# State-space layer: table reads issued from two queues, transposes and GLU items in another order, more filling products

## Chip, core and metric

One NeuronCore of one Trainium2 chip computes a two-layer decoder trunk in a single launch. The metric is the device time of one execution in microseconds (us), as a median of several runs. The engines are TensorE (PE, with its weight loads as PEld), VectorE (DVE), ScalarE (ACT), GpSimd (POOL) and SyncE (SP, which issues the DMA transfers). Each works through its own queue in order and waits for the others by semaphores.

## What is computed

Layer 0 mixes the 512 positions with a diagonal complex state-space layer (64 groups of 16 channels, 64 states each), layer 1 with stick-breaking attention. Each mixer is followed by a layer norm, a dense SwiGLU block and another layer norm. All is float32. The change lies in layer 0's mixer:

```python
def s5_mixer(x, a_re, a_im, log_dt, b_re, b_im, c_re, c_im, d_skip, w_glu, w_out):
    ...
    _, _, s_re, s_im = lax.associative_scan(
        _ssm_combine, (a_seq_re, a_seq_im, bu_re, bu_im), axis=0)
    y = (jnp.einsum('lbgp,ghp->blgh', s_re, c_re.astype(f32))
         - jnp.einsum('lbgp,ghp->blgh', s_im, c_im.astype(f32)))
    y = y.reshape(bsz, seq, D_MODEL) + d_skip.astype(f32) * x.astype(f32)
    h = jax.nn.gelu(y).astype(x.dtype)
    val, gate = jnp.split(h @ w_glu, 2, axis=-1)
    z = val * jax.nn.sigmoid(gate)
    return (z @ w_out).astype(x.dtype)
```

## The kernel before

Layer 0's mixer is `ssm` (L460), and `ssm_end` (L897) finishes its GLU and output projection. The scan over 512 positions is cut into 64 chunks of 8. The 64 groups are handled in four blocks, 0 to 3, of 16 groups (two halves of 8). The instructions of all engines are issued in an order written out by hand, the string `SSM_ORDER` (L61), inside a manual schedule (L875): each word is one step, its first letter the kind and its digit the block. Every engine executes its own instructions in just that order. For one block b:

- **c** (L607): two short copies on ACT that put tables into PSUM bank 1. **g**, **j** (`f_g`, L624): DVE's outer products with B, two halves. **h**, **i** (`f_h`, L629): the same with C. Each half is three DVE operations over 1024 columns.
- **t**, **T** (`p_t`, L634): eight PE transposes of one half of g, and two ACT copies to SBUF, each of one bank. t uses banks 0 and 2, T uses banks 0 and 3. **m**, **M** (`p_m`, L646): PE products of x with the transposed tables, into banks 2 and 3.
- **e** (`f_e`, L713): POOL builds rotation tables (six operations, one into a scratch tile "eu"), ACT one copy. **r** (L735) and **s** (L747): DVE rotates m's result, scans it, rotates back.
- **k** (`p_k`, L667): PE products that give the convolution tables, two ACT copies, and two DMAs that write them to DRAM. **n** (`f_n`, L701): 16 DMAs from SP read them back in shifted form: eight for the block's first eight groups, eight for the others. n needs k's write.
- **y** (`p_y`, L763): PE products of tables and states into banks 6 and 7, a group pair after the other; the first four pairs read only the first half of n's tables. Two ACT copies. **z** (`p_z`, L787): eight PE transposes of that result in banks 6 and 7, GELU on ACT (two operations), and ACT's high part xh. **l** (`f_l`, L801): DVE's low part xl.
- **d9** (`p_d`, L657): nine products of the identity with itself, into bank 7, which nobody reads. They only keep PE at work.
- **u** (`glu_some`, L856): the next item of `GLU_FIRST` (L57): part of the product h @ w_glu on PE in banks 6 (value) and 7 (gate), and two ACT copies that keep it (`glu_keep`, L826). An item "30" is output chunk 3 with input quarter 0 (the rows of block 0); "001" is chunk 0 with quarters 0 and 1, so twice as long. Quarter b needs block b's xh and xl. **w0**, **w4** do the last two items of the list and leave them in PSUM. **a** (`glu_add`, L831) adds kept parts pairwise on POOL.
- **p**, **q** (`pump`, L865): split the next weight chunk into a high part (ACT) and a low part (POOL for p, DVE for q, L231), free its raw buffer, and issue from SP the load of a chunk three further on.

Every tile of 128 x 1024 is taken from a ring of 37 buffers (`Ring`, L160): `get` takes the buffer that has been free the longest in program order, `put` appends one to that list. A new tile waits until the last reader of the former tile in its buffer is done, on whatever engine that is. So the order of the words also decides which tile waits for whom.

In the order before, block 3's h takes the buffer of e3's scratch "eu". The words around it are `u1 u1 u1 a p e3 s2 g3 y2 t3 j3 z2 T3 m3 M3 h3 p u1 i3 p l2 k3 n3 r3 u1 u1 p s3 q y3`.

Of the kernel before, what the change touches and what calls it, by code (L numbers as in the profile page):

```python
# [45 lines left out]
def glu_items(text):  # L46
# [12 lines left out]


SSM_ORDER = (  # L61
# [3 lines left out]
)  # L65

TNX = {0: 0, 1: 1, 2: 0}
# [177 lines left out]
class Trunk:  # L245
# [214 lines left out]
    def ssm(self):  # L460


        tc, nc, io, ring, ws = self.tc, self.nc, self.io, self.ring, self.ws
# [52 lines left out]
        for hf in range(4):  # L516
# [4 lines left out]
        kd = dr.tile([NBLK, 16, 32, 240], F32, name="kd")  # L521
# [4 lines left out]
                          in_=zero.unsqueeze(1).to_broadcast([128, NBLK * 4, 112]))  # L526
# [33 lines left out]
        nr, den, t1, t2, t3, t4, cfr, cfi = (small(n) for n in ("nr", "den", "t1", "t2", "t3", "t4", "cfr", "cfi"))  # L560
        l1, l2 = small("l1"), small("l2")
# [39 lines left out]
        h3 = lambda t, i: t[:, i * 512:(i + 1) * 512].rearrange("p (j c) -> p j c", j=GB)  # L601
# [99 lines left out]
        def f_n(b):  # L701
            if b in TNX:
                half = (self.xl, self.xh)[TNX[b]][:, 4:8].rearrange("p k t -> p (k t)").bitcast(F32)
                tn = [half[:, :1024], half[:, 1024:]]
            else:
                tn = [ring.get("tn", F32) for _ in range(2)]
            for hf in range(2):
                for n in range(L):
                    nc.sync.dma_start(out=tn[hf][n * 16:(n + 1) * 16].rearrange("p (g t) -> p g t", g=8),
                                      in_=kd[b, hf * 8:hf * 8 + 8, 0:16, n * 16:n * 16 + 128].rearrange("g h t -> h g t"))  # L710
            st[b]["tn"] = tn

        def f_e(b):  # L713
# [90 lines left out]

        part, zt = {}, [None] * 8

        def glu(i, qs, banks, start=True, stop=True):

            w = []
            for q in qs:  # L810
                c, half = self.c_glu[i, q]
                hl = ws.get(c, 0)
                w.append([t[:, half * 512:(half + 1) * 512].rearrange("p (k v m) -> p k v m", k=2, v=2) for t in hl])
            for v in (1, 0):
                for n, q in enumerate(qs):
                    for k in range(2):
                        kt = 2 * q + k
                        self.mm3(self.ps[:, banks + v], w[n][0][:, k, v], w[n][1][:, k, v], self.xh[:, kt], self.xl[:, kt],
                                 n == 0 and k == 0 and start, n == len(qs) - 1 and k == 1 and stop)
            for q in qs:  # L820
                c, half = self.c_glu[i, q]
                if half == 1:
                    ws.done(c)

        def glu_keep(i, banks):
            t = ring.get("part", F32)  # L826
            for v in (1, 0):
                nc.scalar.activation(t[:, v * S:v * S + S], self.ps[:, banks + v], AF.Copy)
            part.setdefault(i, []).append(t)

# [24 lines left out]
        def glu_some(n):  # L855
            for _ in range(n):  # L856
                i, qs = first.pop(0)
                glu(i, qs, 6)
                glu_keep(i, 6)

        def rest(banks):
            i, qs = first.pop(0)
            glu(i, qs, banks, stop=False)

        def pump(e):  # L865
# [4 lines left out]
        fs = dict(c=a_c, g=f_g, j=lambda b: f_g(b, 1), h=f_h, i=lambda b: f_h(b, 1), d=p_d, t=p_t,  # L870
                  T=lambda b: p_t(b, 1), m=p_m, M=lambda b: p_m(b, 1), e=f_e, k=p_k, r=f_r, y=p_y, l=f_l,
                  L=lambda b: f_l(b, G_), n=f_n, s=f_s, z=p_z,
                  B=lambda b: (powers(rest_), G_.memset(scr[0][:, 0:1], 0.0), scr_done()), b=lambda b: (levels(rest_), scr_done()))
        ET = mybir.EngineType
        with tc.manual_schedule(engines={ET.PE, ET.DVE, ET.Activation, ET.Pool, ET.SP}):  # L875
            for w in SSM_ORDER.split():
                if w[0] == "u":
                    glu_some(1)
                elif w[0] == "w":
                    rest(int(w[1]))  # L880
                elif w == "x":
                    ws.load(2)
                elif w == "a":
                    glu_add()
                elif w in "pq":
                    pump(G_ if w == "p" else V)
                else:
                    fs[w[0]](int(w[1]))
# [4 lines left out]
        nc.sync.dma_start(out=self.xres, in_=io["x_rev"])  # L893
        self.ln_load(io["ln_mix_g"][0], io["ln_mix_b"][0])
        self.glu, self.glu_end, self.zt = glu, glu_end, zt

    def ssm_end(self, nxt):  # L897
# [349 lines left out]
```

## Time and profile before

| | us |
|---|---|
| median of 3 runs (lowest to highest) | 1248.86 (1248.78 to 1250.04) |
| the profiled execution | 1248.96 |
| its span from first to last instruction | 1247.2 |
| PE busy | 1191.5 |
| DVE, ACT, POOL busy | 666.4, 422.6, 190.5 |

The trace is that of one execution. Its times count from the start of the span; what the device time has beyond the span is the time around it. A timeline row gives an instruction's start and duration, the engine, the line, what it writes and reads, how many were merged, and in brackets how long the engine stood idle before it and what released it. The state-space part takes about the first 205 us; the fields of the table by stretches stand in its header row.

### The profile page before, as it was taken

The page shows a single profiled execution, that of the slowest core. Times are in us where ns is not written, and L with a number is a line of the kernel's source. Part 1 is how long each engine was busy: PE and PEld are TensorE (multiplying, and loading weights), DVE is VectorE, ACT ScalarE, POOL GpSimd, SP SyncE. Part 2 cuts the span into 40 slices and gives each one's busy share as a digit, 9 for nine tenths or more (in the row PEclk, how much of TensorE's full clock was granted, in tenths as well). Part 3 has the DMA queues.
Part 4 walks back from the last instruction along what each step waited for, and adds up shares of the span by engine and source line. Part 5 has one row for each costly group of instructions (what it writes and reads, how often), then busy time and mean ns, then how long its engine had stood idle before and what let it go on. Part 6 is the DMA issues. An engine that isn't in the chain of part 4 may idle for free.

```text
span 1247.2 us, 16906 instructions
## 1 busy us (share of the span) xinstructions
PE 1191.5 (96%) x6964; PEld 989.7 (79%) x6964; DVE 666.4 (53%) x1033; ACT 422.6 (34%) x601; POOL 190.5 (15%) x212
## 2 busy tenths in 40 slices
PE   3799999999999999999999999999999999999996
PEld 2577688898888888888887888878888888888885
DVE  8975666643323333234867787868433333333236
ACT  1355263142222222222246666653222223332200
POOL 6636302120000000001312222224200000000000
PEclk9899999999999999999999999999999999999998
DMA  5333453142222223442201122133322222234301
GB/s 192 111 94 92 144 195 112 37 149 69 85 85 85 85 84 106 148 136 84 85 7 63 52 68 62 58 101 122 133 85 85 85 85 85 69 117 152 102 17 51
DMA packets 44781, 117.66 MB, mean 94 GB/s; under 512 B 6816, under 2 KB 18080, under 8 KB 44576
## 3 DMA queue, kind: packets, MB, share of 16 engines
q1 hardware_dynamic: 44704, 116.59, 29.3%
q8 instruction: 54, 0.88, 0.3%
q14 instruction: 23, 0.19, 0.1%
HBM read 112.51 MB, written 4.06 MB: 93 GB/s over the span
## 4 chain that ended last, share of the span: by engine, by line
PE 83%; DVE 9%; ACT 3%; POOL 2%; issue 1%; DMA 1%; SPq 1%; DVEq 0%; POOLq 0%; ACTq 0%
PE psum L294 17%; PE psum L292 17%; PE psum L293 16%; PE psum L313 8%; PE psum L312 8%; PE psum L311 8%; PE psum L776 2%; DVE nb L1015 2%; PE psum L1037 1%; DVE h L466 1%; ACT wh L228 1%; DVE wl L231 1%; PE psum L1102 1%; PE psum L1053 1%; PE psum L687 1%
## 5 line engine op out<-in xcount | busy, mean ns | idle before, releaser
L292 PE MATMUL psum<-xh,wh 128*128 128x512 f32 (+1 forms) x1056 | 394.6, 374 | 0.8 <-ACT xh L287 0.8
L294 PE MATMUL psum<-xl,wh 128*128 128x512 f32 (+1 forms) x1056 | 393.6, 374 | 0.0
L293 PE MATMUL psum<-xh,wl 128*128 128x512 f32 (+1 forms) x1056 | 391.9, 372 | 0.0
L228 ACT ACTIVATE wh<-raw 128x1024 fp32r<-128x1024 f32 x188 | 194.5, 1055 | 228.4 <-PE psum L313 68.5
L231 DVE TENSOR_TENSOR wl<-raw,wh 128x1024 fp32r<-128x1024 f32 x158 | 196.7, 1274 | 131.7 <-ACT wh L228 103.8
L292 PEld LDWEIGHTS psum<-xh,wh 128*128 128x128 f32 x1056 | 198.4, 188 | 38.7 <-issue 3.0
L293 PEld LDWEIGHTS psum<-xh,wl 128*128 128x128 f32 x1056 | 198.4, 188 | 35.4
L294 PEld LDWEIGHTS psum<-xl,wh 128*128 128x128 f32 x1056 | 197.9, 188 | 33.5
L410 DVE TENSOR_TENSOR s<-s,psum 128x512 f32<-128x512 f32 x44 | 30.3, 688 | 278.9 <-PE psum L294 278.9
L231 POOL TENSOR_TENSOR wl<-raw,wh 128x1024 fp32r<-128x1024 f32 x30 | 74.1, 2485 | 512.6 <-DMA raw<-w_v 317.2
L313 PE MATMUL psum<-wh,hid 128*128 128x512 f32 x352 | 137.6, 391 | 0.0
L312 PE MATMUL psum<-wl,hid 128*128 128x512 f32 x352 | 137.4, 390 | 0.0
L311 PE MATMUL psum<-wh,hid 128*128 128x512 f32 x352 | 137.3, 390 | 0.0
L287 ACT ACTIVATE hid<-s 128x512 fp32r<-128x512 f32 x44 | 27.7, 629 | 172.4 <-DVE s L410 172.4
L313 PEld LDWEIGHTS psum<-wh,hid 128*128 128x128 f32 x352 | 66.1, 188 | 14.2
L312 PEld LDWEIGHTS psum<-wl,hid 128*128 128x128 f32 x352 | 66.1, 188 | 14.0
L311 PEld LDWEIGHTS psum<-wh,hid 128*128 128x128 f32 x352 | 66.1, 188 | 13.5
L1016 POOL TENSOR_TENSOR be<-be,nb 128x768 f32<-128x768 f32 (+1 forms) x24 | 49.5, 2062 | 98.2 <-DVE nb L1015 70.9
L1015 DVE TENSOR_TENSOR_SCAN nb<-nb,dm 128x384 f32<-128x384 f32 (+1 forms) x48 | 50.2, 1088 | 9.7 <-ACT nb L1010 6.9
L409 ACT ACTIVATE s<-psum 128x512 f32<-128x512 f32 x44 | 26.2, 596 | 76.9 <-PE psum L294 76.8
L288 DVE TENSOR_TENSOR hid<-s,hid 128x512 fp32r<-128x512 f32 x44 | 30.5, 693 | 31.9 <-ACT hid L287 31.9
L287 ACT ACTIVATE xh<-psum 128x512 fp32r<-128x512 f32 x24 | 14.0, 596 | 97.1 <-PE psum L357 93.7
(181 smaller groups left out, 1399.8 us busy)
## 6 DMA issues: line engine op xcount, KB each, us to landing
raw<-w_gu SPq DMA_DIRECT2D x88, 512.0 KB, 3.6
raw<-w_down SPq DMA_DIRECT2D x44, 512.0 KB, 3.6
raw<-w_glu SPq DMA_DIRECT2D x16, 512.0 KB, 4.5
raw<-w_qk SPq DMA_DIRECT2D x16, 512.0 KB, 3.6
raw<-w_out SPq DMA_DIRECT2D x8, 512.0 KB, 3.7
raw<-w_v SPq DMA_DIRECT2D x8, 512.0 KB, 3.6
raw<-w_o SPq DMA_DIRECT2D x8, 512.0 KB, 3.6
xres<-xs SPq DMA_DIRECT2D x4, 512.0 KB, 6.9
```

Source lines behind the costliest of these rows:

```text
L228: nc.scalar.activation(h, w, AF.Copy)
L231: (self.l_eng or nc.vector).tensor_tensor(out=l, in0=w, in1=h.bitcast(F32), op=SUB)
L287: self.nc.scalar.activation(h, src, AF.Copy)
L288: self.nc.vector.tensor_tensor(out=l, in0=src, in1=h.bitcast(F32), op=SUB)
L292: mm(out=out, lhsT=sh, rhs=mh, start=first, stop=False)
L293: mm(out=out, lhsT=sl, rhs=mh, start=False, stop=False)
L294: mm(out=out, lhsT=sh, rhs=ml, start=False, stop=last)
L311: mm(out=o, lhsT=sh[:, ts], rhs=hl[0][:, c], start=first, stop=False)
L312: mm(out=o, lhsT=sh[:, ts], rhs=hl[1][:, c], start=False, stop=False)
L313: mm(out=o, lhsT=sl[:, ts], rhs=hl[0][:, c], start=False, stop=last)
L1015: V.tensor_tensor_scan(nb[:, h], nb[:, h], dm[u], 0.0, MUL, ADD)
L1016: G_.tensor_tensor(out=be, in0=be, in1=nb, op=MUL)
```

## The change

It has four parts, all in `ssm`. For block 0, the eight reads of the second half of n go out from ACT's queue and not from SP's. `SSM_ORDER` is rewritten: seven d9 and not two around r0; t ahead of z in block 0, and T too ahead of z in blocks 1 to 3; k, n and a p in blocks 2 and 3 ahead of the item that stood before them; l behind r; e3 ahead of its p. The items u compute and copy the value half first and the gate half second, where it was the other way round; the last items and `ssm_end` keep their order.

```diff
--- before.py
+++ after.py
@@ -59,9 +59,9 @@
 
 
 SSM_ORDER = (
-    "x c0 e0 g0 j0 t0 h0 T0 b0 i0 m0 M0 k0 n0 d9 r0 d9 s0 B0 c1 p e1 y0 g1 z0 t1 j1 T1 m1 M1 h1 p l0 u1 i1 c2 e2 p "
-    "u1 k1 n1 r1 u1 p u1 u1 s1 g2 y1 t2 j2 z1 T2 m2 M2 h2 p u1 i2 c3 l1 p k2 n2 r2 u1 u1 u1 a p e3 s2 g3 y2 t3 j3 "
-    "z2 T3 m3 M3 h3 p u1 i3 p l2 k3 n3 r3 u1 u1 p s3 q y3 q w0 z3 a w4 l3 q q q"
+    "x c0 e0 g0 j0 t0 h0 T0 b0 i0 m0 M0 k0 n0 d9 d9 d9 r0 d9 d9 d9 d9 s0 B0 c1 p e1 y0 g1 t1 z0 j1 T1 m1 M1 h1 p l0 "
+    "u1 i1 c2 e2 p u1 k1 n1 r1 u1 p u1 u1 s1 g2 y1 j2 t2 T2 z1 m2 M2 h2 p i2 c3 k2 n2 p u1 r2 l1 u1 u1 u1 a e3 p s2 "
+    "g3 y2 j3 t3 T3 z2 m3 M3 h3 p i3 k3 n3 p u1 r3 l2 u1 u1 s3 p q y3 q w0 z3 a w4 l3 q q q"
 )
 
 TNX = {0: 0, 1: 1, 2: 0}
@@ -706,8 +706,9 @@
                 tn = [ring.get("tn", F32) for _ in range(2)]
             for hf in range(2):
                 for n in range(L):
-                    nc.sync.dma_start(out=tn[hf][n * 16:(n + 1) * 16].rearrange("p (g t) -> p g t", g=8),
-                                      in_=kd[b, hf * 8:hf * 8 + 8, 0:16, n * 16:n * 16 + 128].rearrange("g h t -> h g t"))
+                    (nc.scalar if b == 0 and hf else nc.sync).dma_start(
+                        out=tn[hf][n * 16:(n + 1) * 16].rearrange("p (g t) -> p g t", g=8),
+                        in_=kd[b, hf * 8:hf * 8 + 8, 0:16, n * 16:n * 16 + 128].rearrange("g h t -> h g t"))
             st[b]["tn"] = tn
 
         def f_e(b):
@@ -804,14 +805,14 @@
 
         part, zt = {}, [None] * 8
 
-        def glu(i, qs, banks, start=True, stop=True):
+        def glu(i, qs, banks, start=True, stop=True, vs=(1, 0)):
 
             w = []
             for q in qs:
                 c, half = self.c_glu[i, q]
                 hl = ws.get(c, 0)
                 w.append([t[:, half * 512:(half + 1) * 512].rearrange("p (k v m) -> p k v m", k=2, v=2) for t in hl])
-            for v in (1, 0):
+            for v in vs:
                 for n, q in enumerate(qs):
                     for k in range(2):
                         kt = 2 * q + k
@@ -824,7 +825,7 @@
 
         def glu_keep(i, banks):
             t = ring.get("part", F32)
-            for v in (1, 0):
+            for v in (0, 1):
                 nc.scalar.activation(t[:, v * S:v * S + S], self.ps[:, banks + v], AF.Copy)
             part.setdefault(i, []).append(t)
 
@@ -855,7 +856,7 @@
         def glu_some(n):
             for _ in range(n):
                 i, qs = first.pop(0)
-                glu(i, qs, 6)
+                glu(i, qs, 6, vs=(0, 1))
                 glu_keep(i, 6)
 
         def rest(banks):
```

## Rows read from the trace of the kernel before

**Rows 1.** The page's first lines: span; busy us, share of the span, instructions.

```profile
span 1247.2 us, 16906 instructions
...
PE 1191.5 (96%) x6964; PEld 989.7 (79%) x6964; DVE 666.4 (53%) x1033; ACT 422.6 (34%) x601; POOL 190.5 (15%) x212
```

**Rows 2.** Stretches: busy per engine in the header's order, granted clock, DMA share, GB/s.

```profile
core 0: us, PE busy (x) PEld busy (x) DVE busy (x) ACT busy (x) POOL busy (x), PEclk, DMA share, GB/s
...
40.10:45.20 5.10, 5.09 (x38) 3.12 (x40) 4.23 (x14) 0.50 (x3) 0.41 (x2) 0.50 0.80 218
...
130.60:134.20 3.60, 3.57 (x129) 3.24 (x129) 3.60 (x2) 0.00 (x0) 1.52 (x1) 0.54 0.02 5
...
153.80:205.00 51.20, 51.20 (x230) 42.09 (x229) 36.08 (x45) 30.21 (x38) 4.55 (x3) 1.00 0.57 193
```

**Rows 3.** The fillers' line, L660: duration ns min/median/max, first and last start us.

```profile
L660 PE MATMUL psum<-ident x36: 275/275/377, 31.3 to 35.3; 128*128 128x128 f32 x36
```

**Rows 4.** PE's timeline: start us, us, line, operation, tiles, count, [idle before <-releaser].

```profile
40.11 0.70 PE L776 MATMUL psum<-xl,xres 128*64 128x128 f32 x4 [4.51 <-DMA xl<-kd]
...
60.32 0.50 PE L292 MATMUL psum<-xh,wh 128*128 128x512 f32 x1
```

**Rows 5.** PE's timeline, blocks 1 and 2.

```profile
77.73 0.44 PE L776 MATMUL psum<-xh,xres 128*64 128x128 f32 x4 [0.69 <-DMA xh<-kd]
...
85.36 1.09 PE L642 MATMUL psum<-ident,g 128*128 128x128 f32 x8
...
91.57 1.15 PE L653 MATMUL psum<-xres,gt 128*64 128x64 f32 x32 [2.29 <-ACT gt L643]
...
92.66 0.50 PE L292 MATMUL psum<-xh,wh 128*128 128x512 f32 x1
...
95.62 0.32 PE L687 MATMUL psum<-cc,g 64*32 64x16 f32 x16
...
107.32 0.44 PE L776 MATMUL psum<-xl,xres 128*64 128x128 f32 x4 [0.69 <-ACT part L828]
```

**Rows 6.** SP's timeline, DMA issues of block 0's table reads.

```profile
34.13 7.43 SPq L709 DMA_DIRECT2D xl<-kd  x16
```

**Rows 7.** ACT's timeline, blocks 0 to 2.

```profile
44.67 0.28 ACT L611 ACTIVATE psum<-pk 128x128 f32<-128x128 f32 x1 [12.59 <-DVE pk L466]
...
86.05 1.09 ACT L643 ACTIVATE gt<-psum 128x512 f32<-128x512 f32 x2
...
89.49 1.06 ACT L799 ACTIVATE xh<-hg 128x1024 fp32r<-128x1024 f32 x1
...
98.21 0.66 ACT L695 ACTIVATE ksb<-psum 128x256 f32<-128x256 f32 x2 [0.43 <-PE psum L687]
```

**Rows 8.** DVE's timeline, blocks 1 to 3.

```profile
90.58 1.23 DVE L466 TENSOR_TENSOR xl<-hg,xh 128x1024 fp32r<-128x1024 f32 x1 [4.34 <-ACT xh L799]
...
92.84 1.22 DVE L466 TENSOR_TENSOR w<-e,psum 128x1024 f32<-128x1024 f32 x1 [1.04 <-PE psum L653]
...
96.57 2.30 DVE L752 TENSOR_TENSOR_SCAN psum<-r,psum 128x1024 f32<-128x1024 f32 x1
...
123.42 1.22 DVE L466 TENSOR_TENSOR h<-psum,cc 128x1024 f32<-128x1024 f32 x1 [7.76 <-POOL e L466]
...
130.49 2.71 DVE L466 TENSOR_TENSOR xl<-hg,xh 128x1024 fp32r<-128x1024 f32 x1
```

**Rows 9.** PE's timeline, block 3 from k3 to y3.

```profile
130.63 0.41 PE L687 MATMUL psum<-h,g 64*32 64x112 f32 x8 [2.00 <-DVE h L466]
...
134.17 0.54 PE L292 MATMUL psum<-xh,wh 128*128 128x512 f32 x1
...
146.17 0.44 PE L776 MATMUL psum<-tn,xres 128*64 128x128 f32 x4 [0.69 <-ACT part L828]
```

**Rows 10.** POOL's timeline, blocks 2 and 3.

```profile
107.34 6.98 POOL L466 TENSOR_TENSOR part<-part,part 128x1024 f32<-128x1024 f32 x3 [7.07 <-ACT part L828]
...
129.77 2.35 POOL L231 TENSOR_TENSOR wl<-raw,wh 128x1024 fp32r<-128x1024 f32 x1 [3.97 <-ACT wh L228]
```

## The prediction

> **What bounds the kernel now.** I read the page's counters first: PE is busy for 1191.5 of 1247.2 us [rows 1], so time can only be won or lost where PE stands still, runs at half clock or does work that nobody needs. The table by stretches says where that is: from 153.80 us on, when block 3's output product y3 has ended, PE is busy for 51.20 of 51.20 us; before it there are holes, and behind two of them stretches at a granted clock of 0.50 and 0.54, the first all and the second nearly all at the 1.2 GHz level [rows 2]. Everything that the diff touches lies ahead of 153.80. So I follow one number through the four blocks, the **start of y3, now 146.17**; what it moves by, the end moves by, since PE's work behind it stays the same and has no slack. Timelines of PE, ACT, DVE and POOL give the steps.
>
> **Block 0: the filling products.** Two d9 (18 products) appear as 36 instructions, starting from 31.3 to 35.3 at full clock: 4.0 / 35 = 0.114 us each [rows 3]. Now PE waits 4.51 us for tables, and y0 starts at 40.11 with the clock halved until 45.2 [rows 2, 4]. Seven d9 are 126 instructions: 126 x 0.114 = 14.4 us, and y0 stands behind them in PE's queue. It starts at 31.3 + 14.4 = **45.7 us**, 5.6 later, but at full clock. The order behind it (t1, z0, T1, m1, M1) is the one that block 1 already has, so block 1's rows price it: from y1's start at 77.73 to the first GLU product at 92.66 it is 14.93 [rows 5]. 45.7 + 14.93 = 60.65, against 60.32 now [rows 4]: **+0.3 us**. The warm clock and the transposes' new place give back what the fillers cost.
>
> **The transfers on ACT.** SP issues block 0's 16 table reads in 7.43 us, 0.46 each [rows 6]. With eight on ACT, the second half lands some 3.7 us sooner. Nobody waits for it: y0's first four groups read only the first half, still issued by SP, and PE now arrives at 45.7. I take no gain. The cost: no row shows a DMA issued by ACT. At SP's price it is 3.7 us of ACT, from 34.1; behind them in ACT's queue stand c1's two table copies, which now start at 44.67 after 12.59 us of idle [rows 7]. That covers up to 10.6 / 8 = 1.3 us each. At twice that, c1 and g1 would move by 10.6 us and t1 by about 5 (g1 and j1 have a few us to spare); I take SP's price, the only one of a DMA issue here, so nothing. The weight loads behind SP's reads go out 3.7 us earlier; the next split is not late now, so again nothing.
>
> **Block 1.** The chain through u1, k1 and table transfers keeps its lengths, so y1 starts at 78.06. DVE's l0 now waits for ACT's split behind the later y0: 5.6 us later, less the 2.5 that 5.1 us at half clock cost, so DVE falls back by about 3.1; in block 1 it stands idle for 4.34 and 1.04 us now [rows 8], which covers it. Now T2's copies stand on ACT behind block 1's GELU and its split (ending at 90.55), and M2 waits 2.29 us for them [rows 5, 7]. With T2 ahead of z1, they follow t2's copies directly. What is late next is T2 itself: it needs the bank that t2's first copy empties (86.05 + half of 1.09 [rows 7]), about 0.35 us after t2 ends. M2 starts at 91.57 - 2.29 + 0.35 + 0.33 = 89.95 and ends at 91.05, **1.6 us earlier** than now.
>
> **Block 2.** Between M2 and y2 PE has k2 and four items in both orders; k2 comes first now, its inputs being long ready, and its tables are then read well ahead of y2. The new order of GLU halves (gate's bank last) lets y2 begin in the first bank while the second is being copied: the 0.69 us wait at y2 [rows 5] goes; so does the one at y3 [rows 9]; with the semaphore steps I take 0.9 and 0.85. y2 starts at 107.32 - 1.6 - 0.9 = 104.75, **2.6 earlier**. Moving l1 behind r2 puts 1.2 us ahead of s2, but r2 starts 1.6 us sooner, so s2 is no later than now, when y2 waited for ACT and not for it.
>
> **Block 3: the order that costs.** POOL starts adding kept GLU parts when the last of the items is copied: 107.34 now [rows 10], 105.5 then. The three adds (6.98), e3 and the split follow in either order, and DVE's h3 waits for POOL: now 7.76 us, until 123.42, because h3's buffer is the one e3's scratch leaves [rows 8, 10]. Following the ring's free list through the new order, h3 gets the buffer of the weight chunk that POOL's split reads, and that split now stands *behind* e3. The same 16.1 us pass: h3 starts at 121.6, and k3, which needs h3 and i3 (123.42 to 130.63, 7.2 us [rows 8, 9]), at **128.8**, 1.8 earlier. But what PE does meanwhile changes. Now the item "001" stands between M3 and k3 and fills 5.6 us of that wait (an item's length, below); then it stands behind k3. PE is done with M3 at 104.75 + 7.63 (y) + 5.35 (t to M) = 117.7 and has nothing for 11.1 us. After k3 come three items, not two. Now k3 takes from 130.63 to 134.17, cold, and two items plus the wait take until 146.17: (12.0 - 0.69) / 2 = 5.65 each [rows 9]. So y3 starts at 128.8 + 3.54 + 3 x 5.65 = **149.3**. z2's GELU now waits for e3's scratch, until one split (2.35 [rows 10]) before 121.6; that lies inside the hole. n3's reads end long before y3.
>
> **Sum**, against the profiled execution of 1248.96 (span 1247.2 plus 1.76 around it; 0.1 above the median): 149.3 - 146.17 = +3.1, so 1252.1. The halved clock after an 11 us hole is bounded by rows on both sides: after 4.5 us of idle the clock came back 5.1 us into the work, in k3's place 3.6 [rows 2]; the first would make up to 1.6 us of the first item run at half speed (+0.8), a k3 at full speed (2.6, as k2 from 95.62 to 98.21 [rows 5, 7]) would take 0.95 less. I add 0.1, since k3's own row already is a cold one: **1252.2 us**.
>
> **A page against a row.** DVE's xl split takes 1.23 us alone at 90.58, and 2.71 beside a POOL split that had begun 0.72 us before it [rows 8, 10]. In the new order l1 starts when r2 is through, 91.2 + 3.7 = 94.9 (92.84 to 96.57 [rows 8]), and POOL's split of chunk 5 starts behind k2 (2.6), its copies (0.66) and a 1.06 us ACT split: 91.05 + 4.3 = 95.35 [rows 5, 7].
> The Trainium skill (SBUF — State Buffer, section "Who interferes with whom") says that a VectorE instruction with two SBUF inputs and a GpSimd one that reads SBUF exclude each other for the whole instruction, and whichever starts first wins. By that rule l1 loses nothing if it is really first, and POOL waits; the rows here show only the case of POOL first.
>
> **Rivals.** (a) *POOL wins that race*: the margin is 0.45 us. l1 would end about 1.1 us after POOL's split (as 133.2 against 132.1 [rows 8, 10]), near 98.8; u7, due at 96.3, waits 2.5, and everything behind moves: 1254.7. For it: the small margin; against it: both start times follow from M2, so they shift together. Chance 0.10. (b) *The clock survives or returns at once in block 3*: k3 at 2.6 us instead of 3.54 takes the sum to 1251.2, within the measurement's reach. For it: behind 2.29 us of idle, M2 still ran 32 instructions in 1.09 us, a warm pace [rows 5]; against: 4.5 us of idle ended it [rows 2]. Chance 0.16. (c) *Faster*: h3's buffer is free early. One mechanism in one place: if it were a buffer that POOL doesn't read last, h3 would start with j3's end, which is now 123.42 - 7.76 = 115.66 and then 1.8 + 2.3 earlier (j3's own buffer comes with the first add, not the second), 111.5; k3 at 118.7, y3 at 139.2, the total 1242. It decides as soon as h3 starts before 119. Against it: the same free list, followed through the old order, names e3's scratch as h3's buffer, and the row shows h3 waiting for just that. Chance 0.12. (d) *The ACT transfers do nothing*: that is in the forecast.
>
> **How the numbers follow.** Forecast 0.62, its own range 1250.9 to 1253.6 (clock bounds, and half a microsecond for each hand-over); (a) 0.10; (b) 0.16; (c) 0.12. About 0.2% (2.5 us) is what a measurement of this kernel can tell from no change, so the line is at 1251.4. Some 0.14 of the forecast's chance lies below it. Slower: 0.48 + 0.10 = 0.58; same: 0.16 + 0.14 = 0.30; faster 0.12. The range reaches from (b) to (a): 1250.0 to 1255.0, and leaves (c) out.
>
> **What would show it.** 126 filler instructions ending near 45.7 and y0 taking 7.6 us; u1 within 0.5 us of 60.6; M2 without a long wait for ACT; k2 ahead of the item; y2 near 104.8; DVE's longest wait on POOL's split, to about 121.6; PE idle for some 11 us before k3, then three items, and y3 near 149.3. An h3 ahead of 119, or a y3 ahead of 146, would make it wrong; so would a gap in PE behind y3 that could absorb the shift.

## The result and the profile after

The changed kernel takes **1256.17 us** (median of 6 runs, 1254.76 to 1257.02) where the kernel before, on the same chips, takes 1248.88 (6 runs, 1246.73 to 1250.04): a ratio of 1.0058, 95% interval 1.0045 to 1.0071. The side was foreseen, slower; the size was not: +7.3 us instead of +3.3, outside the range of 1250.0 to 1255.0. The profiled execution is one of 1256.94 us. Its page, as [rows 1]:

```profile
span 1255.1 us, 17084 instructions
...
PE 1199.8 (96%) x7054; PEld 999.0 (80%) x7054; DVE 665.2 (53%) x1033; ACT 423.0 (34%) x601; POOL 190.5 (15%) x212
```

The start of y3 moved from 146.17 to 154.50, 8.33 later; the execution is 7.98 longer. So the method of following y3 held, and everything that was missed lies ahead of it. PE's timeline of the changed kernel, with the rows that answer to [rows 4, 5, 9]:

```profile
45.59 0.44 PE L777 MATMUL psum<-xl,xres 128*64 128x128 f32 x4
...
59.45 1.98 PE L653 MATMUL psum<-xres,gt 128*64 128x64 f32 x32 [2.31 <-ACT gt L643]
61.35 0.80 PE L292 MATMUL psum<-xh,wh 128*128 128x512 f32 x1
...
67.57 0.32 PE L687 MATMUL psum<-cc,g 64*32 64x16 f32 x16
...
71.57 0.38 PE L687 MATMUL psum<-h,g 64*32 64x112 f32 x3 [1.50 <-issue]
71.88 0.50 PE L292 MATMUL psum<-xh,wh 128*128 128x512 f32 x1
...
81.39 0.44 PE L777 MATMUL psum<-xh,xres 128*64 128x128 f32 x4 [0.99 <-DMA xh<-kd]
...
94.27 0.32 PE L687 MATMUL psum<-cc,g 64*32 64x16 f32 x16
...
97.91 0.38 PE L687 MATMUL psum<-h,g 64*32 64x112 f32 x4 [1.13 <-issue]
98.22 0.50 PE L292 MATMUL psum<-xh,wh 128*128 128x512 f32 x1
...
109.42 0.44 PE L777 MATMUL psum<-xl,xres 128*64 128x128 f32 x4
...
133.49 0.60 PE L687 MATMUL psum<-h,g 64*32 64x112 f32 x8 [2.93 <-DVE h L466]
...
145.13 0.50 PE L294 MATMUL psum<-xl,wh 128*128 128x512 f32 x1 [0.15 <-DVE xl L466]
...
154.50 0.44 PE L777 MATMUL psum<-tn,xres 128*64 128x128 f32 x4
```

Read from the top. y0 starts at 45.59, as forecast. M1 starts when forecast, but its 32 products take 1.98 where M2 before, behind the same idle time, took 1.09 [rows 5]. In k1 and again in k2, three or four products before the end, there is a wait that the trace of before doesn't have: 1.50 and 1.13, released by "issue", which means that nothing in the profile was waited for. M2 and y2 wait for nobody, as forecast. The table by stretches has the clock:

```profile
core 0: us, PE busy (x) PEld busy (x) DVE busy (x) ACT busy (x) POOL busy (x), PEclk, DMA share, GB/s
45.60:53.20 7.60, 7.60 (x97) 4.87 (x96) 7.53 (x7) 2.21 (x3) 6.84 (x6) 1.00 0.43 142
...
57.20:59.40 2.20, 0.00 (x0) 0.00 (x0) 0.94 (x1) 2.17 (x5) 0.00 (x0) 0.93 0.00 0
59.45:61.40 1.95, 1.95 (x33) 1.83 (x33) 1.95 (x3) 0.89 (x1) 0.98 (x1) 0.50 0.00 0
...
133.49:137.20 3.71, 3.71 (x128) 3.39 (x128) 0.00 (x0) 0.00 (x0) 0.00 (x0) 0.50 0.02 4
154.50:205.70 51.20, 51.20 (x291) 40.75 (x291) 33.16 (x39) 29.08 (x36) 8.01 (x3) 1.00 0.53 183
```

y0 runs at full clock; M1 ran at 0.50, the 1.2 GHz level, behind 2.31 us without work, and so did the start of the item behind it. POOL's timeline of the changed kernel, and behind it DVE's, against [rows 8, 10]:

```profile
110.20 6.99 POOL L466 TENSOR_TENSOR part<-part,part 128x1024 f32<-128x1024 f32 x3 [7.79 <-ACT part L829]
```

```profile
126.28 1.23 DVE L466 TENSOR_TENSOR h<-psum,cc 128x1024 f32<-128x1024 f32 x1 [10.07 <-POOL wl L231]
...
140.26 1.22 DVE L466 TENSOR_TENSOR w<-e,psum 128x1024 f32<-128x1024 f32 x1 [6.83 <-DMA kd<-ksb]
...
143.86 1.22 DVE L466 TENSOR_TENSOR xl<-hg,xh 128x1024 fp32r<-128x1024 f32 x1
```

h3 waits for POOL's split and starts 16.1 us after POOL's adds, as forecast to a tenth. New is the second row: r3 stands still for 6.83 us, because its tile w was given the buffer of k3's ksb and so waits for the DMA that writes ksb out; l2, now behind r3, comes at 143.86, and the item that needs it waits. SP and ACT issue block 0's reads together, against 0.46 us each for SP alone [rows 6]: 5.29 / 8 = 0.66 and 5.62 / 8 = 0.70. SP's timeline, and behind it ACT's:

```profile
34.14 5.29 SPq L709 DMA_DIRECT2D xl<-kd  x8
```

```profile
34.72 5.62 ACTq L709 DMA_DIRECT2D xl<-kd  x8
```

### The profile page after: what moved, and what is told of

Read it like the earlier page. It is cut to its first block, busy times and chain, and to the rows that moved or that the text cites. A ratio compares the mean times of both kernels' runs of the same rounds, so it can differ in the third digit from the quotient of the medians.

```text
span 1255.1 us, 17084 instructions
## 1 busy us (share of the span) xinstructions
PE 1199.8 (96%) x7054; PEld 999.0 (80%) x7054; DVE 665.2 (53%) x1033; ACT 423.0 (34%) x601; POOL 190.5 (15%) x212
## 4 chain that ended last, share of the span: by engine, by line
PE 84%; DVE 9%; ACT 2%; issue 2%; POOL 2%; DMA 1%; SPq 0%; DVEq 0%; POOLq 0%; ACTq 0%
PE psum L294 16%; PE psum L292 16%; PE psum L293 16%; PE psum L312 8%; PE psum L313 8%; PE psum L311 8%; PE psum L777 2%; DVE nb L1016 2%; PE psum L660 1%; PE psum L1038 1%; PE psum L687 1%; DVE h L466 1%; DVE wl L231 1%; ACT wh L228 1%; PE psum L1103 1%
```

## The experiments

All runs in one table; "stops" are the waits for "issue" inside k1 and k2. Times are medians; ratio and 95% interval are to the kernel before on the same chip (medians 1248.4 to 1248.9 there).

| run | us | ratio | u1 | y2 | y3 | stops in k1, k2 |
|---|---|---|---|---|---|---|
| before | 1248.88 | 1 | 60.32 | 107.32 | 146.17 | none |
| after | 1256.17 | 1.0058 [1.0045, 1.0071] | 61.35 | 109.42 | 154.50 | 1.50, 1.13 |
| e1_lead54 | 1253.88 | 1.0039 [1.0027, 1.0052] | 61.12 | 105.29 | 150.43 | none |
| e2_before_lead45 | 1250.31 | 1.0014 [1.0003, 1.0025] | 60.36 | 110.41 | 147.79 | 1.16, 0 |
| e3_item_back | 1255.58 | 1.0052 [1.0039, 1.0065] | 60.49 | 108.86 | 149.80 | 1.27, 1.11 |
| e4_sp_only | 1256.92 | 1.0063 [1.0051, 1.0076] | 61.97 | 110.08 | 155.16 | 1.19, 1.08 |
| f3_lead64 | 1258.83 | 1.0072 [1.0053, 1.0091] | 63.80 | 111.69 | 156.77 | 0.81, 1.44 |
| f2_two_d9 | 1252.0 | 1.0030 [1.0019, 1.0042] | 60.21 | 104.59 | 149.68 | 0, 0.56 |
| g1_two_d9_sp | 1248.73 | 1.0002 [0.9991, 1.0014] | 57.75 | 102.19 | 147.28 | 0, 0.86 |
| g4_four_d9_sp | 1248.47 | 0.9998 [0.9988, 1.0008] | 56.37 | 100.84 | 146.40 | none |
| f4_order_only | 1246.92 | 0.9989 [0.9979, 0.9999] | 60.70 | 105.27 | 145.01 | 0, 0.82 |
| f1_lead_item_l2 | 1247.23 | 0.9988 [0.9978, 0.9998] | 60.66 | 104.69 | 143.16 | none |
| g2_e3_first | 1242.72 | 0.9945 [0.9931, 0.9959] | 61.22 | 105.49 | 138.13 | none |
| g3_best | 1236.98 | 0.9909 [0.9892, 0.9926] | 56.41 | 101.47 | 134.13 | none |

**The stops in k1 and k2.** PE's instructions arrive by a DMA queue of their own, in pieces of 16 KB; the page of the changed kernel names it "instruction" and counts 55 pieces. Twice 7054 PE instructions (products and weight loads) in 55 pieces are some 256 each. Theory F: a k issues 320 instructions in some 2.5 us, faster than the next piece comes, and PE runs dry where a piece ends inside k. Each added product shows as two products and two weight loads, so the 45 are 180 instructions and move every end. Rival Q: the stops have to do with what k waits for. The first test adds products that nobody reads at the very start of PE's queue, where PE is idle, so that only the ends of the pieces move:

```diff
-    "x c0 e0 ...
+    "d9 d9 d9 d9 d9 d9 x c0 e0 ...
```

> The changed kernel with 54 more unread products of the identity at the very start of PE's queue, where PE has nothing to do until 18.7 us; nothing else differs. Theory F (instruction supply): PE stood still for 1.7 us inside k1 and 1.4 us inside k2 of the changed kernel with no engine to wait for, because a block of its instruction stream ended there; 216 instructions more in front move both block ends out of k1 and k2. Both stalls go, y3 starts about 3.1 us earlier than 154.5, the time is about 1253.1. Rival Q (queues): the stalls come from the reads issued on ACT or from the new order of k and n; neither is touched, so both stalls stay, y3 at 154.5, time 1256.2.

Both stops are gone and y3 comes 4.1 us earlier (the median falls by 2.3). PE's waits from 60 to 155 us, of the changed kernel and then of this one (waiting line and tile, releaser: us in total, times, longest):

```profile
PE psum L687 <- DVE h L466: 10.1, 2, 7.2
PE psum L687 <- issue: 2.6, 2, 1.5
PE psum L777 <- DMA xh<-kd: 1.0, 1, 1.0
PE psum L642 <- ACT gt L643: 0.6, 2, 0.3
PE psum L294 <- DVE xl L466: 0.2, 1, 0.2
```

```profile
PE psum L687 <- DVE h L466: 10.1, 2, 7.2
PE psum L653 <- ACT gt L643: 2.3, 1, 2.3
PE psum L777 <- ACT part L829: 0.7, 1, 0.7
PE psum L642 <- ACT gt L643: 0.6, 2, 0.3
```

The line "issue" is what vanished (M1's wait is new in the list only because it ends behind 60 here). The stops are worth 3.3 us (k1 and k2 take 2.49 each until the next item, in the changed kernel 4.31 and 3.95). M1 and the item behind it, at full clock this time, give 1.3 (6.79 from M1's start to k1 against 8.12), and y0 took back 0.6: it started at 46.20, having waited 0.59 for its tables. The reverse test puts the 45 products into the kernel before, at the same idle place:

```diff
-    "x c0 e0 ... k0 n0 d9 r0 d9 s0
+    "d9 d9 d9 d9 d9 x c0 e0 ... k0 n0 d9 r0 d9 s0
```

> The kernel before with 45 more unread products (the number that the change adds) at the very start of PE's queue, in idle time; order, queues and fillers ahead of y0 as before. Theory F: the stream is shifted by the same 180 instructions as in the change, so PE stalls near the ends of k1 and k2 by 1.5 to 1.7 us each; y3 moves from 146.2 to about 149.3, time about 1252. Rival Q: no stall, the time of the kernel before, 1248.9.

PE's timeline:

```profile
69.74 0.38 PE L687 MATMUL psum<-h,g 64*32 64x112 f32 x4 [1.16 <-issue]
...
93.12 1.43 PE L653 MATMUL psum<-xres,gt 128*64 128x64 f32 x32 [2.30 <-ACT gt L643]
94.48 0.80 PE L292 MATMUL psum<-xh,wh 128*128 128x512 f32 x1
```

One stop appears, in k1; the second, which I had expected too, does not. Here k2 stands behind an item, whose 24 products took 4.2 us (behind M2's wait the clock had halved, as the last two rows show; before, it took 2.96): the piece was asked for during the item, at 97.21, and was there in time. In the changed kernel the same piece was asked for at 95.25, when k2 was already running. So an end inside k is not enough; the request must also come too late. The same follows from the size: 320 instructions are more than a piece, so an end lies inside every k, also in the kernel before. The 54 products didn't take the ends out of k1 and k2, as I had put it; they moved them from the 313th instruction to about the 97th (313 - 216), and the pieces that begin there had been asked for before k began (one request per end, in order: 56.69 and 87.22, where k1 and k2 start at 66.83 and 91.39). That the late request is the reason is read from these times; no run changes it alone. That the place of the ends decides, a control tests. If the pieces are 256 instructions, then 64 leading products (256 instructions) must bring the stops back to the same places:

```diff
-    "x c0 e0 ...
+    "d9 d9 d9 d9 d9 d9 d9 d1 x c0 e0 ...
```

> The changed kernel with 64 unread products at the start of PE's queue, ten more than in the run with 54: 64 products are 256 instructions, the distance that lay between two ends of the blocks in which the stream arrives. F expects the ends to fall on the same places of k1 and k2 as in the changed kernel, so both stalls come back (1.1 to 1.5 us each, 313 or 314 instructions into k1 and k2), y3 near 154, the time near 1255.5. Rival D (any work at the start helps, by the clock or by a later start of something) expects no stall and 1253.9 or less, as with 54.

PE's timeline:

```profile
73.63 0.38 PE L687 MATMUL psum<-h,g 64*32 64x112 f32 x3 [0.81 <-issue]
...
100.19 0.38 PE L687 MATMUL psum<-h,g 64*32 64x112 f32 x3 [1.44 <-issue]
```

They are back. Counted in the trace (to within two), PE stopped behind its 1473rd and 2241st instruction in the changed kernel (and in e3 and e4), behind the 1473rd in e2, behind the 1729th and 2497th here, and behind the 1985th in f2, f4 and g1: all of them differ by multiples of 256. So F holds in this form: what decides is where the ends of the pieces lie and whether the next one was asked for in time. The profiled execution (1258.78) is above what I expected because block 0 itself was late: the stretches of k0 and of the first fillers had a granted clock of 0.72 and 0.81, and y0 started at 48.15. From y0 to y3 it is 108.6 us, as in the changed kernel (108.9), against 104.2 with 54; of the 4.4 between the last two, 2.9 are the stops and 1.5 the clock behind M1's wait.
The Trainium skill (Runtime: NRT & Kernel Launch, section "Instruction fetch mechanics") describes just these blocks of 256 instructions and says that the cost of crossing one is mostly hidden; the rows agree on the size and show what is not hidden, 0.6 to 1.5 us at the twelve stops of the table, all in a stage as dense as k.

**The transfers on ACT.**

```diff
-                    (nc.scalar if b == 0 and hf else nc.sync).dma_start(
+                    nc.sync.dma_start(
```

> The changed kernel with all 16 reads of block 0 issued from SP again. My theory: PE reaches y0 at 45.7 behind the fillers, when either half has landed, so the time is unchanged, 1256.2 within 1. Rival Q: the reads on ACT's queue disturb PE or the later reads; then the stalls in k1 and k2 shrink and the time falls by 2 to 3 us.

Nothing moves (y0 and y3 are both 0.6 to 0.7 later, as the whole of block 0 was), as expected of a transfer that the fillers hide, and both stops stay, so the reads on ACT's queue don't cause them. The cover is thin: with reads on two queues and seven d9, y0 still waited 0.59 and 0.70 us for tables in e1 and g2. And a hidden cost is still a cost, as the fillers cut back to before's two showed:

```diff
-n0 d9 d9 d9 r0 d9 d9 d9 d9 s0
+n0 d9 r0 d9 s0
```

> The changed kernel with before's two d9 instead of seven: 45 products fewer, y0 near 40 at half clock, and PE's instruction stream 180 records shorter. F expects k1's stall gone; k2 begins 19 records behind the end of an instruction block, so a small stall of at most 0.6 us there; u1 near 60.3 to 60.8; y3 near 154.5 - 1.5 - 0.8 - 0.8 = 151.4, the time near 1253.5. If the fillers pay for themselves by the clock (rival W: warm engine through block 0), u1 comes at 63 or later and the time stays at 1256.

u1 (60.21) and the small stop in k2 (0.56) came as expected; y0 did not. (y3 was 1.7 earlier than expected, half of that because M1 and the item behind it ran at full clock.) PE's timeline of this run, and behind it its DMA view of the reads (last figure: median us from issue to landing):

```profile
43.03 0.69 PE L777 MATMUL psum<-xl,xres 128*64 128x128 f32 x4 [7.44 <-DMA xl<-kd]
```

```profile
xl<-kd SPq DMA_DIRECT2D x8, 64.0 KB, 3.7
xl<-kd ACTq DMA_DIRECT2D x8, 64.0 KB, 3.8
```

So I took ACT's part away here as well (e4's edit on top of f2's):

> The run with two d9 (1252.0) with all 16 reads of block 0 issued by SP again. There y0 started at 43.03, behind 7.44 us of waiting for tables, 2.6 to 2.9 us later than in the runs whose reads all come from SP (40.1 and 40.45). Theory A (eight reads issued by ACT at the same time make the first half land later; the fillers only hide it) expects y0 at 40.1 to 40.5. T1 then waits for DVE's j1, near 52.7, so u1 comes near 58.2 instead of 60.21, y3 near 147.7 instead of 149.68 and the time near 1250.0. Rival B (the reads' landing has another cause, such as the weight loads) expects y0 near 43 and 1252.

The same two views of this run:

```profile
40.65 0.70 PE L777 MATMUL psum<-xl,xres 128*64 128x128 f32 x4 [4.78 <-DMA xl<-kd]
```

```profile
xl<-kd SPq DMA_DIRECT2D x16, 64.0 KB, 2.3
```

Theory A stands: with all 16 on SP the first half, on which y0 waits, is there 2.4 us sooner; y3 comes 2.4 earlier, and the median is 3.3 lower. Two queues finish issuing sooner (5.4 against 7.4 us), but each read takes 3.7 us to land and not 2.3, and the eighth read of the first half goes out later.
The Trainium skill (DMA: Bandwidth & Descriptors, section "Issuing engines are not separate DMA queues") says that issuing from several engines saves only the time of issuing; the rows agree, and add that the part which is needed first can lose by it.

**The number of fillers.**

```diff
-n0 d9 d9 d9 r0 d9 d9 d9 d9 s0
+n0 d9 d9 r0 d9 d9 s0
...
-                    (nc.scalar if b == 0 and hf else nc.sync).dma_start(
+                    nc.sync.dma_start(
```

> The changed kernel with four d9 instead of seven, and all reads issued by SP. Four d9 end at 31.3 + 72 x 0.114 = 39.5, before the tables land, so y0 should start at 40.1 to 40.5 and run warm; t1 then waits for g1 (49.1) and T1 for j1 (52.7): u1 near 58.2 instead of 61.35. The stream is 108 instructions shorter than in the changed kernel, so F expects no stall in k1 and k2. y3 near 147.5, the time near 1250.0. If seven d9 are the right number (rival W: fewer of them leave the engine cold), u1 stays above 60 and the time above 1252.

y0 started at 40.27 and at full clock, with one wait of 1.06 us in its middle, at the fifth group pair, the first to read the second half of the tables (the trace names a weight load as what ended it, so what held it stays open). u1 came at 56.37, even earlier than expected, because M1 waited only 0.57 for its copies; no stop; and the time is that of the kernel before. Set against the changed kernel, y3 comes 8.1 us earlier, of which 5.0 are won by u1 (the three d9 too many and M1's clock) and most of the rest by the stops. Against the runs of the long fillers in which M1 was warm and y0 started right behind the fillers (e3 and f1, u1 at 60.49 and 60.66), the three d9 alone are 4.1 to 4.3, where y0 starts 5.3 and 5.5 later.

**Block 3.** The item back into its place between M3 and k3:

```diff
-h3 p i3 k3 n3 p u1 r3 l2 u1 u1 s3
+h3 p u1 i3 k3 n3 p r3 l2 u1 u1 s3
```

> The changed kernel with one item, 001, put back between M3 and k3, where the kernel before has it. Theory H (the hole in block 3): PE fills 5.5 us of its 11 us hole, k3 still starts near 133.5 since POOL's split decides h3, and two items and not three follow it; r3 no longer waits for k3's write, so the 0.5 us wait of the second item for l2 goes too. y3 near 148.4, time about 1250. Rival: the hole is harmless because something else (table reads, l2, DVE's s3) is late at y3; then the gain is under 2 us, time above 1254.

y3 moved by 4.7 of the 6 us expected, 4.1 of it behind y2. The last items now waited for l2, which stood behind r3, and r3 waited until k3 was done (135.14). The item put back started 3.59 us late, too: z2's GELU must empty its banks first, and the GELU waits for e3's scratch on POOL, as the prediction said of it. PE's timeline:

```profile
125.48 0.79 PE L292 MATMUL psum<-xh,wh 128*128 128x512 f32 x1 [3.59 <-ACT hg L797]
...
140.43 0.50 PE L294 MATMUL psum<-xl,wh 128*128 128x512 f32 x1 [3.16 <-DVE xl L466]
```

Yet the profiled execution gained only 2.3 (1254.66 against 1256.94), and the median 0.6. The profile shows where 2.7 went: in the attention layer, behind a hole of 1.73 us, the work from L1038 to the next wait took 32.1 us (653.91 to 686.02), in the changed kernel 29.4 (658.33 to 687.74), at a granted clock of 0.54 against 1.00. M1 of e3 ran warm, but the item behind it did not, so k1 started no earlier than in the changed kernel (67.73 against 67.57). The stretches of e3, behind M1 and behind the hole, and then the changed kernel's behind its hole (columns as above):

```profile
60.49:63.90 3.41, 3.41 (x12) 2.74 (x9) 3.38 (x4) 0.45 (x1) 3.41 (x3) 0.51 0.00 0
...
653.90:660.00 6.10, 6.09 (x27) 5.30 (x28) 4.11 (x8) 3.47 (x7) 2.12 (x4) 0.54 0.17 27
```

```profile
658.30:664.40 6.10, 6.07 (x42) 5.00 (x43) 5.45 (x9) 4.51 (x8) 2.45 (x5) 1.00 0.28 86
```

How often that happened in this kernel's other executions no trace shows, so why its median gained so little stays open; by the time alone (1255.58), the rival of the expectation would have it. With l2 ahead of k3 as well, and the 54 leading products, the three causes are undone together:

```diff
-    "x c0 e0 ...
+    "d9 d9 d9 d9 d9 d9 x c0 e0 ...
...
-h3 p i3 k3 n3 p u1 r3 l2 u1 u1 s3
+h3 p u1 i3 l2 k3 n3 p r3 u1 u1 s3
```

> The changed kernel with three repairs: 54 unread products at the very start of PE's queue (so that blocks of PE's instruction stream end elsewhere), the item 001 back between M3 and k3, and l2 ahead of k3. Theory F (PE's instruction supply stalls k1 and k2, the item's place costs block 3 its cover, l2 behind r3 makes the last items wait) expects the sum: y3 at 150.4 (with the 54 alone) less what the item's return gave when it was moved alone (154.5 - 149.8 = 4.7, of which about 0.9 was a warm M1) less the 3.2 us that the item then waited for l2: near 143.5, so a time near 1245.5. If the item's return gives nothing in the end (rival N: the time is set by something behind y3), the time stays at the 1253.9 of the 54 products alone.

y3 at 143.16 (143.5 expected); the profiled execution took 1245.86 (1245.5 expected), the median is 1247.23. So the sum holds at y3, with other terms than I had given it: against e1, 6.7 us are won between y2 and y3, of which the item gives 4.1, as in e3, and l2 2.5 and not 3.2; and e3's 4.7 held no gain from a warm M1. The gains that the prediction saw, alone on the kernel before:

```diff
-g2 y1 t2 j2 z1 T2 m2 M2 h2 p u1 i2 c3 l1 p k2 n2 r2 u1 u1 u1 a p e3 s2 g3 y2 t3 j3 z2 T3
+g2 y1 j2 t2 T2 z1 m2 M2 h2 p i2 c3 k2 n2 p u1 r2 l1 u1 u1 u1 a p e3 s2 g3 y2 j3 t3 T3 z2
...
-                glu(i, qs, 6)
+                glu(i, qs, 6, vs=(0, 1))
```

> The kernel before with only what the prediction held for gains: T ahead of z in blocks 1 to 3, k2 ahead of its item, l1 behind r2, and the value half of the GLU items first; before's block 0, its order a p e3, and its item and l2 ahead of k3. The prediction's steps expect M2 1.6 us earlier, y2 2.6 earlier (104.7), y3 3.4 earlier (142.7): 1245.4. F adds that k2 now starts 27 instructions earlier in the stream, 19 behind the end of a block: a stall of at most 0.6 in k2, so 1245.4 to 1246.0. Rival N (what is won ahead of y3 is lost behind it, or h3 keeps its place) expects y2 early but y3 within 1 us of 146.2: 1248.

1246.92: a gain, but half of what I expected, between the theory and rival N. y2 came 2.05 earlier (the stop in k2 took the rest), y3 only 1.16: I had let y2's gain go on to y3, though k3 waits for h3 and h3 for POOL, whose chain begins with the last item's copy and came only 1.3 sooner. DVE's timeline:

```profile
122.15 1.23 DVE L466 TENSOR_TENSOR h<-psum,cc 128x1024 f32<-128x1024 f32 x1 [10.09 <-POOL e L466]
```

**A version that beats both.** So POOL's chain binds block 3. e3 reads no kept part and needn't stand behind the adds. First that alone on top of f1, then with g4's block 0 in place of the leading products:

```diff
-u1 r2 l1 u1 u1 u1 a e3 p s2
+u1 r2 l1 u1 u1 u1 e3 a p s2
```

> The run with 54 leading products, the item and l2 ahead of k3 (1247.23, y3 at 143.16), with e3 ahead of a in POOL's queue as well. There POOL stood idle until 105.47, when the last item's copy let its adds begin, and DVE's h3 waited 10.07 us, to 121.55, for a split that stands behind the adds and e3. e3 needs no part: it can run from 98.9 on, 6.7 us of it inside POOL's idle time. Theory P (block 3 is bound by POOL's chain of adds, e3 and split) expects h3 near 115, y3 near 137 and a time near 1241. Rival N (something else holds block 3 by then: M3's end near 117.7, or z2) expects y3 no earlier than 141, 1245 or more.

> The same with block 0 as in the run with four d9 and SP's reads, and no leading products (the shorter stream puts the ends of the instruction blocks at the same places of k1 and k2 as the 54 leading products did, within some ten instructions, so no stall is due). If the parts add up: 137 - 2.4 (block 0) = 134.6 for y3 and a time near 1238.5; if block 3 has another bound, the 2.4 us are lost and the time is that of the run before it.

g2: h3 at 115.80, y3 5.0 earlier, 1242.72. Its profile shows e3's stretch in the attention layer again (32.1 us from L1038 to the next wait), so the profiled execution, 1243.5, holds 2.7 us from that; whether the other four (1241.07 to 1242.98) did, no trace shows. g3 takes **1236.98 us**, a ratio of 0.9909 [0.9892, 0.9926], some 0.9% below the kernel before. Its y0 and y3 on PE's timeline, and behind them its h3 on DVE's:

```profile
39.94 0.44 PE L777 MATMUL psum<-xl,xres 128*64 128x128 f32 x4 [0.34 <-DMA xl<-kd]
...
134.13 0.44 PE L777 MATMUL psum<-tn,xres 128*64 128x128 f32 x4
```

```profile
111.80 1.23 DVE L466 TENSOR_TENSOR h<-psum,cc 128x1024 f32<-128x1024 f32 x1 [5.46 <-POOL wl L231]
```

## Why the prediction was right in kind and wrong in size

The forecast of block 3, from which "slower" came, held. What failed lies ahead of it: "the chain through u1, k1 and table transfers keeps its lengths" (with k2 at its old length too), and the warm M1. The steps in order:

- **Block 0** (fillers to 45.7, u1 at 60.65): right up to M1 (45.7 + 14.93 is 60.63, a slip of 0.02). y0 started at 45.59 and ran at full clock, and M1 started at 59.45. The failed step is "block 1's rows price it": those rows hold an M2 that ran warm behind 2.29 us of idle, and so I let M1 run warm. It ran at 0.50, and k1 started 1.2 us later than forecast (67.57 against 60.65 + 5.71 = 66.36). The row was one draw. Behind holes of 2.29 to 2.33 us the clock fell in four of eight traces: M1 took 1.87 to 1.98 in the changed kernel, e4 and f3; in e3 M1 took 1.15, but the item behind it ran cold. From M1's start to k1 it is 8.12 to 8.32 us in these four and 6.79 in the other four (e1, f1, f2, g2). And in e2 the very M2 that the prediction read, in before's order and behind 2.30 us, lost the clock. What decides it, no run shows.
- **"The warm clock and the transposes' new place give back what the fillers cost"**: right as arithmetic, +0.3, but the sum compared seven d9 with two only. Four put u1 at 56.37 (g4), 4.1 to 4.3 us ahead of seven at the same clock; the forecast didn't ask for that.
- **The transfers on ACT** ("I take no gain"): right for this kernel (e4), by cover. Its price per issue, SP's 0.46, was wrong, 0.66 to 0.70 here with both queues at work; and "y0's first four groups read only the first half, still issued by SP" missed that this half lands later. Uncovered, that costs 2.4 us at y0 and at y3, 3.3 in the medians (f2 against g1).
- **Block 1** ("the chain through u1, k1 and table transfers keeps its lengths"): this is the step that failed most. k1 took 4.31 us until the next item and not 2.49: +1.8, for PE's instruction supply, a term that the sum didn't have. The tables came 0.3 later. M2 no longer waited for ACT: from y1 to k2 it is 12.88 us where the forecast's own steps give 12.99.
- **Block 2** (107.32 - 1.6 - 0.9 is 104.82, not 104.75; it moves nothing): k2 ran dry as well, 3.95 against 2.49: +1.5. The new order of the GLU halves did what was forecast: no wait at y2 or y3. y2 came at 109.42, which is 104.75 + 1.2 + 1.8 + 0.3 - 0.1 + 1.5.
- **The page against a row** (l1 beside POOL's split): l1 took 2.01 us beside a split that had begun first, at 96.62, so some 0.8 was lost; but it was another split than the one I named, and the item that needs l1 came later. Nothing hung on it, and rival (a), a race with the split that began at 100.01, didn't come about: l1 was ending then.
- **Block 3**: the mechanism was right. POOL's adds to h3 took 16.1 us, h3 to k3 7.2, and PE stood idle behind M3 for want of the item. The sizes were 0.2 (k3 cold, 3.73 against 3.54) and 0.3 (three items 17.28 against 16.95) too small; half of the second (0.15) is the wait for l2 behind r3 behind ksb's DMA, a hand-over through a buffer that I had not followed for r3.

The sum: 149.3 + 4.7 (up to y2, and unchanged through POOL to k3) + 0.2 + 0.3 = 154.5, where y3 was. Of the 5.2 us missed, 3.3 are the two stops, which were in none of the rivals; the clock is most of the rest. Of the rivals, (c) didn't occur, h3's buffer being what the free list said, and (b) went the other way: the clock fell at a place where I had counted on it.

## What to carry to other kernels

Filler instructions on PE are not free even in idle time: they shift where the 256-instruction pieces of its stream end, and a dense stage of small products can then run dry (3.3 us here); look for waits on "issue" inside such a stage, and move the end with a few leading products before judging an order. Fillers should end just before the data lands: of the 5.3 to 5.5 us by which seven d9 put y0 behind four, 4.1 to 4.3 were still there at u1. Follow the ring's free list for every tile behind a moved step, not only for the one that was late before, and follow a wait to the engine whose chain sets it: putting e3 ahead of POOL's adds was worth 5.0 us at y3 (g2 against f1), where all the gains that the change was made for gave 1.2 (f4).

## What the runs showed of the hardware that I had not expected

- PE stopped for 0.6 to 1.5 us at places a multiple of 256 instructions apart, in a stage where 320 of them pass in 2.5 us. The request for the piece goes out some way ahead (95.25 to 96.53 for the piece on which k2 waited until 97.91, 1.4 us after it had landed).
- Reads issued by SP and ACT together cost 0.66 to 0.83 us each to issue (after and f2 at the low end, e1 at the high one), against 0.46 on SP alone, and landed in 3.7 to 4.6 us instead of 2.3 or 2.4.
- The same hole of PE sometimes halves the clock behind it and sometimes doesn't: 2.3 us at M1 in four traces of eight, 2.3 and 2.4 us at M2 and M3 in e2 but not in the kernel before, and 1.3 to 1.8 us at the attention layer's L1038 in two (e3 and g2, 2.7 us each) of the eleven in which I read it.
